# Products of w_out with two mixers' features beside the delta rule's norm and gate, and the modulation's columns spread anew

## The chip, the cores and the metric

The kernel runs on one core of a Trainium2 chip. The metric is the device time of one execution in microseconds (us). The time before is the median of 3 runs. Where the text speaks of levels of TensorE's clock, it means the granted clock that the profile shows: 1.00 is 2.4 GHz and 0.50 is 1.2 GHz.

## The reference, cut to what matters

The reference runs two blocks over 256 positions of width 1024, in float32. Only the seams that the change touches are shown.

```python
# first block, one layer
z = rms_norm(h, pre_mix_norm) @ w_in
o_rw  = rwkv7_mixer(...)      # delta rule: 384 features, group norm and gate at its end
o_nsa = nsa_mixer(...)        # sparse attention: 384 features
o_s5  = s5_mixer(...)         # state space: 256 features
mix = concatenate([o_rw, o_nsa, o_s5]) @ w_out          # 1024 x 1024
h = h + rms_norm(mix, post_mix_norm)
f = conv_ffn(rms_norm(h, pre_ffn_norm), w_up, conv_w, conv_b, w_down)
h = h + rms_norm(f, post_ffn_norm)
e = rms_norm(p @ w_ple, ple_norm); h = h + sigmoid(h @ w_ple_gate) * e
# second block: 112 columns of 128 modulation values, used as shifts, scales and gates
mod = silu(c) @ ada_w + ada_b       # 2 layers x 48 columns, and 16 for the keys and values
x = x + g1 * pool_mixer(...);  x = x + g2 * conv_ffn(...)      # layer 0
x = x + g1 * dilated_attention(...);  x = x + g2 * conv_ffn(...)  # layer 1
```

## The kernel before, in words

Activations lie transposed: 8 blocks of 128 features on the partitions, 256 positions along the free dimension. A linear layer is computed in three products of float32r halves. Each input is split into a rounded part `R` and a rest `L`, each weight tile `raw` into `wr` (a cast on ScalarE, L214) and `wl` (a difference on VectorE, L215), and `mm3` (L223 to L227) adds wr·R, wr·L and wl·R in one bank of PSUM. One output block of 128 features with 8 input blocks is 24 such instructions. Weights come over SP's queue in tiles of 512 KB, through 4 raw buffers and 2 buffers each of `wr` and `wl` in the mixers' stage.

The order on each engine is not written out by hand: a planner that simulates the engines orders the instructions by priority and readiness; `high_priority` lifts a block, `manual_schedule` keeps an engine's instructions of a block in their written order, and `issue_after(x)` keeps an instruction behind `x` on its engine. Once planned, each engine works strictly in that order.

**The mixers' stage** runs the delta rule (`rwkv`, lifted), the sparse attention (`nsa`) and the state space (`s5`, `s5_out`) beside each other. The delta rule ends in a chain of small products (`uprod`, L1017). Then come its group norm and gate (L689 to L698): `O` is centred by a product with `cen`, squared on ScalarE, summed per head by 12 small products, raised to the power -0.5 on POOL (L1040, 12 columns at once), spread by products (`head_bcast`), and VectorE multiplies by the spread factor (L695), adds `bon` (L696), multiplies by the gate `gv` (L697) and splits into `R[0..2]`, `L[0..2]`. `R[3..5]` are the sparse attention's features, `R[6..7]` the state space's.

**`post`** (L1156) follows with w_out: 8 output blocks, each with all 8 input blocks in turn, beginning with the delta rule's block 0. Of each block ScalarE writes a scaled copy `F` (L1164) and a square (L250); POOL adds the squares up (L254), and only the last two go through a product with ones. `rstd` turns the sums into the norm's factor (L270, POOL's power at L272, a spread by products). Then VectorE scales F and adds it to `xT` (L1175, L1177), each block's squares are summed by products with ones (32 instructions), a second `rstd` follows, and `norm_split` makes the next layer's inputs. The products of `w_ple` (`ple_vec`) and then `w_up` come next.

**The modulation** has 112 columns, which are made beside other work in two ways. `ada(n)` (L1127) loads 512 KB on SP's queue and makes one column by a VectorE instruction over 1024 elements (L1138); hooks call it after each output block at a rate from the tuple `ADA`. `ada_rows(n)` (L1083) makes four columns ("a row") by four loads of 512 KB through 3 buffers `adw` and 64 TensorE instructions, which are planned behind the last linear product; then ScalarE copies the row, two products turn it, and VectorE adds the bias (L1079). `ROWS` says how many rows stand at each place. The order of the columns is fixed: 0 to 63, then 96 to 111, then 64 to 95. `attention_layer` needs columns 104 to 111 for `gk` (L1376), the gain of the inputs `raw_x` of keys and values; `modv` makes at once whatever is missing.

Of the kernel before, what the change touches and what calls it, by code (L numbers as in the profile page):

```python
# [9 lines left out]
F32 = mybir.dt.float32  # L10
# [7 lines left out]
T = 256  # L18
# [10 lines left out]
ADA = (0,.5,2,.5,1.25,2,3.25,.75)  # L29
# [3 lines left out]
SKIP_W, SKIP_R, SKIP_A, SKIP_A2, SKIP_O = 480, 192, 0, 0, 0  # L33
# [7 lines left out]
ROWS = (1,2,0,0,1)  # L41
# [93 lines left out]
class Net:  # L135
# [46 lines left out]
    def setup(self):  # L182
# [10 lines left out]
        self.ones1 = self.const([128, 1], "ones1")  # L193
        nc.vector.memset(self.ones1, 1.0)
        self.mhalf = self.const([128, 12], "mhalf")
        nc.vector.memset(self.mhalf, -0.5)
        self.mod = self.const([128, 112], "mod")
# [3 lines left out]
        self.skip(self.cp, SKIP_W)  # L201
# [158 lines left out]
    def first(self):  # L360
# [11 lines left out]
        self.mixers(self.rstd(st, self.rcol))  # L372

    def mixers(self, rb):
        tc, a = self.tc, self.a
        with tc.tile_pool(name="mx", bufs=1) as mx, tc.tile_pool(name="mxp", bufs=2, space=PSUM) as self.px:
# [10 lines left out]
            if ORDER:  # L387
                self.fillq[0].clear(), self.fillq[1].clear()
                for c in ORDER:
                    if c == "u":  # L390
                        self.mix_u()
                    elif c == "r":
                        with tc.high_priority():
                            self.rwkv()
                    else:
                        for _ in dict(w=self.mix_nsa, s=self.s5, S=self.s5_out, c=self.nsa_cmp, n=self.nsa)[c]():
                            pass
                return
            self.mix_u()
            with tc.high_priority():  # L400
                self.rwkv()
# [89 lines left out]
    def rwkv(self):  # L491
# [45 lines left out]
        inv = self.head_stat(sq, 1.0, 1e-24, ALU.max)  # L537
# [99 lines left out]
        if not ORDER:  # L637
            self.fillq[0].append(self.nsa())
            self.fillq[1].append(self.s5_out())
# [43 lines left out]
        for q in self.fillq:  # L683
            self.drain(q)

        Oc, sq = t3("t4"), t3("sq3")
        for j in range(3):
            pc = rp()
            self.mm(pc[:, 0:T], self.cen, O[:, j])  # L689
            nc.scalar.activation(sq[:, j], pc[:, 0:T], AF.Square)  # L690
            nc.scalar.activation(Oc[:, j], pc[:, 0:T], AF.Identity, scale=self.vcol("rw_gn_w", j))
        inv = self.head_stat(sq, 1.0 / 64, GN_EPS, None)
        for j in range(3):
            ib = self.head_bcast(inv, j)
            nc.vector.tensor_tensor(Oc[:, j], Oc[:, j], ib, op=ALU.mult)  # L695
# [941 lines left out]
```

## Time and profile before

| | us |
|---|---|
| median of 3 runs | 1275.24 |
| lowest and highest | 1268.41, 1276.17 |
| profiled execution | 1271.01 |
| its span | 1269.1 |
| TensorE busy in the span | 1188.2 (94%) |
| VectorE, ScalarE, POOL busy | 940.1, 682.2, 99.8 |
| bytes moved | 247.19 MB |

The profile shows one execution. Its times count from the first instruction to the last; the remaining 1.9 us lie around the span. TensorE's busy time overstates its work where matmuls queue up or the clock is at its lower level, so a stretch is judged by three things together: what TensorE waited for, the granted clock, and the distance from one product to the next.

### The profile page before, as it was taken

The numbers are of one execution on the slowest core, as the hardware profiler recorded it, in microseconds if no ns is written. First come the engines' busy times: TensorE is split into PE (matmuls) and PEld (weight loads), VectorE is DVE, ScalarE is ACT, GpSimd is POOL, SyncE is SP. The second block draws the span as 40 slices with busy tenths as digits, with TensorE's granted clock in tenths as the row PEclk, the third lists the DMA queues.
The fourth block names the chain that finished last, engine by engine and source line by source line (L and its number), as shares of the span: only waits on it lengthen the run. The fifth ranks groups of instructions, "written<-read, shape, count | busy, mean of one in ns | idle before, by whom it ended". The sixth has DMA issues, their size and how long they took to land. (4 is left out here: it accounts for less than half of the span.)

```text
span 1269.1 us, 26242 instructions
## 1 busy us (share of the span) xinstructions
PE 1188.2 (94%) x10574; PEld 1119.6 (88%) x10574; DVE 940.1 (74%) x1847; ACT 682.2 (54%) x1194; POOL 99.8 (8%) x125
## 2 busy tenths in 40 slices
PE   5997899999999988888999998999999999999996
PEld 4985676899999988888999897999999998999996
DVE  7899646479999757788999866757574757877753
ACT  7633634556665535555665546455655466755541
POOL 0023200220000101220000010000000001000010
PEclk9998898889999988989999998999999999999998
DMA  8521300557668774367888783766464633666651
GB/s 282 159 86 51 119 34 4 189 203 256 219 235 299 258 265 160 124 238 260 313 309 283 284 312 116 286 219 218 165 218 151 229 116 106 204 192 203 211 184 34
DMA packets 71547, 247.19 MB, mean 195 GB/s; under 512 B 8192, under 2 KB 10496, under 8 KB 71424
## 3 DMA queue, kind: packets, MB, share of 16 engines
q1 hardware_dynamic: 71136, 244.72, 55.8%
q8 instruction: 83, 1.36, 0.4%
q10 hardware_dynamic: 288, 0.79, 0.2%
q14 instruction: 40, 0.33, 0.1%
HBM read 244.42 MB, written 1.05 MB: 193 GB/s over the span
## 5 line engine op out<-in xcount | busy, mean ns | idle before, releaser
L215 DVE TENSOR_TENSOR wl<-raw,wr 128x1024 fp32r<-128x1024 f32 (+3 forms) x348 | 412.0, 1190 | 145.4 <-ACT wr L214 143.5
L214 ACT CAST wr<-raw 128x1024 fp32r<-128x1024 f32 (+3 forms) x348 | 350.9, 1014 | 303.0 <-PE acc L226 242.9
L225 PE MATMUL acc<-R,wr 128*128 128x256 f32 x1472 | 413.5, 283 | 7.4 <-ACT wr L214 5.6
L227 PE MATMUL acc<-R,wl 128*128 128x256 f32 x1472 | 414.1, 282 | 2.7 <-DVE wl L215 2.6
L226 PE MATMUL acc<-L,wr 128*128 128x256 f32 x1472 | 414.4, 282 | 0.0
L225 PEld LDWEIGHTS acc<-R,wr 128*128 128x128 f32 x1472 | 280.0, 191 | 11.9 <-ACT wr L214 6.1
L227 PEld LDWEIGHTS acc<-R,wl 128*128 128x128 f32 x1472 | 280.0, 191 | 6.0 <-DVE wl L215 3.7
L226 PEld LDWEIGHTS acc<-L,wr 128*128 128x128 f32 x1472 | 282.1, 192 | 2.1 <-issue 1.4
L227 PE MATMUL acc<-aR,wl 128*128 128x256 f32 x608 | 168.6, 280 | 7.0 <-DVE wl L215 7.0
L225 PE MATMUL acc<-aR,wr 128*128 128x256 f32 x608 | 167.7, 281 | 6.0 <-ACT aR L282 5.3
L226 PE MATMUL acc<-aL,wr 128*128 128x256 f32 x608 | 168.6, 280 | 0.5 <-DVE aL L283 0.5
L1138 DVE SCALAR_TENSOR_TENSOR adw<-adw,cond 128x1024 f32<-128x1024 f32 x96 | 117.5, 1228 | 37.4 <-DMA adw<-in_ada_dram 36.0
L227 PEld LDWEIGHTS acc<-aR,wl 128*128 128x128 f32 x608 | 114.9, 190 | 8.0 <-DVE wl L215 8.0
L254 POOL TENSOR_TENSOR sq<-sq,sq 128x256 f32<-128x256 f32 x48 | 51.2, 1066 | 892.5 <-ACT sq L250 585.0
L225 PEld LDWEIGHTS acc<-aR,wr 128*128 128x128 f32 x608 | 114.4, 190 | 6.6 <-ACT aR L282 5.4
L226 PEld LDWEIGHTS acc<-aL,wr 128*128 128x128 f32 x608 | 115.7, 191 | 0.7 <-DVE aL L283 0.7
L225 PE MATMUL acc<-raw_x,wr 128*128 128x256 f32 (+1 forms) x320 | 92.5, 289 | 2.0 <-ACT wr L214 1.0
L226 PE MATMUL acc<-raw_x,wr 128*128 128x256 f32 (+1 forms) x320 | 92.6, 289 | 1.6 <-DVE raw_x L319 1.5
L227 PE MATMUL acc<-raw_x,wl 128*128 128x256 f32 (+1 forms) x320 | 92.6, 290 | 0.8 <-DVE wl L215 0.7
L242 PE MATMUL acc<-wr,raw_x 128*128 128x256 f32 x384 | 68.7, 281 | 0.4 <-DVE V L1439 0.4
L227 PEld LDWEIGHTS acc<-raw_x,wl 128*128 128x128 f32 x320 | 61.9, 194 | 2.7 <-issue 1.5
L225 PEld LDWEIGHTS acc<-raw_x,wr 128*128 128x128 f32 x320 | 61.5, 192 | 3.1 <-ACT raw_x L318 1.5
(416 smaller groups left out, 1711.8 us busy)
## 6 DMA issues: line engine op xcount, KB each, us to landing
adw<-in_ada_dram SPq DMA_DIRECT2D x96, 512.0 KB, 5.8
raw<-in_ffn_w_up_dram SPq DMA_DIRECT2D x88, 512.0 KB, 4.4
raw<-in_w_up_dram SPq DMA_DIRECT2D x44, 512.0 KB, 3.9
raw<-in_ffn_w_down_dram SPq DMA_DIRECT2D x32, 512.0 KB, 4.5
raw<-in_attn_w_q_dram SPq DMA_DIRECT2D x24, 512.0 KB, 6.7
raw<-in_w_k_dram SPq DMA_DIRECT2D x24, 512.0 KB, 3.6
raw<-in_w_v_dram SPq DMA_DIRECT2D x24, 512.0 KB, 3.9
raw<-in_w_in_dram SPq DMA_DIRECT2D x19, 512.0 KB, 3.6
```

The lines of the kernel that those rows point to most:

```text
L214: nc.scalar.copy(wr, raw)
L215: nc.vector.tensor_sub(wl, raw, wr[:].bitcast(F32))
L225: mm(out, wr, xr, start=start, stop=False)
L226: mm(out, wr, xl, start=False, stop=False)
L227: self.last_mm = mm(out, wl, xr, start=False, stop=stop).ins
L242: self.nc.tensor.matmul(out, lhsT, rhs, start=start, stop=stop)
L254: nc.gpsimd.tensor_tensor(sq, sq, self.sqsum, op=ALU.add)
L1138: nc.vector.scalar_tensor_tensor(w, w, 1.0, self.cond, op0=ALU.mult, op1=ALU.mult, accum_out=self.mod[:, i:i + 1])
```

## The change

The products with w_out leave `post` and move into a new function `mix_out` within the mixers' stage. Four banks of PSUM hold the eight output blocks, two to a bank. The products with input blocks 6, 7 and 3 of outputs 0 to 3 (`a67`, `a3`), then of outputs 4 to 7 (`b67`, `b3`), then those with blocks 4 and 5 (`k4`, `k5`) are placed between the steps of the delta rule's norm and gate; those with blocks 0 to 2 (`c`) come last, two outputs at a time. The weights are loaded in 12 pieces of other shapes, whose rows are 512 to 1536 bytes long; six are split into the two wr/wl buffers and six into tiles whose last use by the delta rule lies before. The gate's product is drawn ahead (bon·gv and Oc·gv before the factor is there), POOL's power is taken in three instructions of 4 columns, and the squares of all eight outputs are summed by products with ones (`pre=False`). Modulation: `ADA` is lower in the second block's first FFN and its w_down (1.25 to 1, 2 to 1.5 per output) and in the attention (3.25 to 3), there are two rows in place of one ahead of the attention, and the last FFN makes half a column per output. Pools `mx`, `mxp` and `wpm` get `reuse_waits="tile"`, a pad is gone, and `rawt` is 32 columns longer.

```diff
-ADA = (0,.5,2,.5,1.25,2,3.25,.75)
+ADA = (0,.5,2,.5,1,1.5,3,.75,.5)
-ROWS = (1,2,0,0,1)
+ROWS = (1,2,0,0,2)
...
-        with tc.tile_pool(name="mx", bufs=1) as mx, tc.tile_pool(name="mxp", bufs=2, space=PSUM) as self.px:
+        with tc.tile_pool(name="mx", bufs=1, reuse_waits="tile") as mx, tc.tile_pool(name="mxp", bufs=2, space=PSUM, reuse_waits="tile") as self.px:
...
+    def mix_out(self):
...
+        pz = [self.psum("acc", self.nacc) for _ in range(2)] + [self.psum("ms", MSB) for _ in range(2)]
+
+        def weights(m0, mn, k0, kn, tags=None):
+            n = mn * kn * 128
+            raw = self.rawload(self.a["w_out"][m0:m0 + mn, :, k0 * 128:(k0 + kn) * 128].rearrange(
+                "m p (k f) -> p m k f", k=kn), [128, mn, kn, 128])
+            if tags is None:
+                wr, wl = (self.wp.tile([128, mn, kn, 128], F32R, name=self.uid(t), tag=t, bufs=self.nw)[:] for t in ("wr", "wl"))
+            else:
+                w = [self.mxt([128, n * 2 // len(tags)], t, F32R) for t in tags]
+                wr, wl = (t.rearrange("p (m k f) -> p m k f", m=mn, k=kn) for t in (w[0][:, 0:n], w[-1][:, -n:]))
+            nc.scalar.copy(wr, raw)
+            nc.vector.tensor_sub(wl, raw, wr.bitcast(F32))
+            return wr, wl, m0, mn, k0, kn
+
+        out = lambda m: pz[m // 2][:, m % 2 * T:(m % 2 + 1) * T]
+
+        def products(w, m, ks=None):
+            wr, wl, m0, _, k0, kn = w
+            for k in range(kn):
+                self.mm3(out(m), wr[:, m - m0, k], wl[:, m - m0, k], self.R[:, k0 + k], self.L[:, k0 + k],
+                         k0 + k == 6 and m % 2 == 0, k0 + k == 2 and m % 2 == 1)
+
+        def early(w, anchor):
+            with tc.issue_after(anchor):
+                for m in range(w[2], w[2] + w[3]):
+                    products(w, m)
+
+        a67, a3 = weights(0, 4, 6, 2), weights(0, 4, 3, 1)
+        c = [weights(0, 2, 0, 3, ("e0", "e1")), weights(2, 2, 0, 3, ("t6", "Kt"))]
+        nc.vector.tensor_tensor(bon, bon, gv, op=ALU.mult)
+        early(a67, self.chain)
+        Oc, sq = t3("t4"), t3("sq3")
+        with tc.high_priority():
+            for j in range(3):
+                pc = self.psum("mx", 2)
+                last = nc.tensor.matmul(pc[:, 0:T], self.cen, O[:, j], start=True, stop=True).ins
+                nc.scalar.activation(sq[:, j], pc[:, 0:T], AF.Square)
+                nc.scalar.activation(Oc[:, j], pc[:, 0:T], AF.Identity, scale=self.vcol("rw_gn_w", j))
+        early(a3, last)
+        with tc.high_priority():
+            v, last = self.head_sums(sq, 1.0 / 64, GN_EPS)
+        nc.vector.tensor_tensor(Oc, Oc, gv, op=ALU.mult)
+        k4 = [weights(0, 4, 4, 1, ("t0", "t1")), weights(4, 4, 4, 1, ("t2", "t5"))]
+        c += [weights(4, 2, 0, 3, ("PB",)), weights(6, 2, 0, 3, ("PK",))]
+        b67, b3 = weights(4, 4, 6, 2), weights(4, 4, 3, 1)
+        early(b67, last)
+        early(b3, last)
+        with tc.manual_schedule(engines={mybir.EngineType.DVE}):
+            inv = self.tmp([128, 2, 6], "hr")
+            for j in range(3):
+                with tc.high_priority():
+                    h = slice(2 * j, 2 * j + 2)
+                    nc.gpsimd.tensor_tensor(inv[:, :, h], v[:].rearrange("p (a h) -> p a h", a=2)[:, :, h],
+                                            self.mhalf[:, 0:4].rearrange("p (a h) -> p a h", a=2), op=ALU.pow)
+            for j in range(3):
+                with tc.high_priority():
+                    ib = self.head_bcast(inv[:].rearrange("p a h -> p (a h)"), j)
+                    nc.vector.tensor_tensor(Oc[:, j], Oc[:, j], ib, op=ALU.mult)
+                    nc.vector.tensor_tensor(Oc[:, j], Oc[:, j], bon[:, j], op=ALU.add)
+                    self.split(Oc[:, j], self.R[:, j], self.L[:, j])
+            k5 = [weights(4 * i, 4, 5, 1) for i in range(2)]
+        for w in k4 + k5:
+            early(w, self.last_bc)
...
+        F = self.mxt([128, KB, T], "z9")
+        st = self.psum("st", 1)
+        for m in range(KB):
+            if m % 2 == 0:
+                products(c[m // 2], m)
+                products(c[m // 2], m + 1)
+            nc.scalar.activation(F[:, m], out(m), AF.Identity, scale=self.vcol("post_mix_norm", m))
+            self.sq_stat(st, out(m), m, pre=False)
+        return self.post_add(F, self.rstd(st[:, 0:2]), True)
...
-        self.ffn_up(a["ffn_w_up1"], None, False, "ffn_conv_w_2", "ffn_conv_b_2", 1, ps)
+        self.ffn_up(a["ffn_w_up1"], lambda m: self.ada(ADA[8]), False, "ffn_conv_w_2", "ffn_conv_b_2", 1, ps)
...
-        with tc.tile_pool(name="wo", bufs=1, reuse_waits="tile") as n.fp:
-            st = n.post(a["w_out"], n.R, n.L, n.vcol("post_mix_norm", 0, 8), KB, stat=True)
...
-    n.rawt = rt.tile([128, KB, 2, T + 32], F32R, name="raw_x")
+    n.rawt = rt.tile([128, KB, 2, T + 64], F32R, name="raw_x")
```

`post_add` is the second half of `post` before (L1171 to L1186), unchanged in what it does.

## Rows read from the trace of the kernel before

**Rows 1.** Page: busy time, share of the span, instructions of TensorE.
```profile
PE 1188.2 (94%) x10574; PEld 1119.6 (88%) x10574; DVE 940.1 (74%) x1847; ACT 682.2 (54%) x1194; POOL 99.8 (8%) x125
```

**Rows 2.** Stretches: length, busy time of each engine, granted clock, DMA share, GB/s.
```profile
206.50:213.00 6.50, 6.50 (x54) 4.95 (x50) 1.73 (x4) 3.72 (x10) 0.00 (x0) 1.00 0.01 3
213.00:215.60 2.60, 0.01 (x1) 0.00 (x0) 0.17 (x1) 0.00 (x0) 2.30 (x3) 0.67 0.01 3
215.60:224.10 8.50, 8.30 (x46) 7.28 (x47) 4.78 (x14) 3.56 (x5) 0.08 (x2) 0.50 0.10 31
224.10:243.90 19.80, 19.76 (x172) 19.55 (x172) 7.36 (x6) 10.93 (x20) 6.14 (x6) 1.00 0.46 161
243.90:248.80 4.90, 1.88 (x15) 1.52 (x14) 1.55 (x5) 1.17 (x3) 0.71 (x1) 0.92 0.70 245
248.80:256.00 7.20, 6.97 (x32) 6.88 (x32) 4.91 (x14) 3.85 (x8) 0.00 (x0) 0.50 0.51 199
```

**Rows 3.** Timeline of POOL: start, length, instruction, and the idle time before it.
```profile
213.30 2.28 POOL L1040 TENSOR_TENSOR hr<-hv,mhalf 128x12 f32<-128x12 f32 x1 [66.33 <-DVE hv L1036]
...
245.83 0.71 POOL L272 TENSOR_TENSOR rr<-rv,mhalf 128x2 f32<-128x2 f32 x1 [2.78 <-DVE rv L270]
```

**Rows 4.** Timeline of TensorE between the delta rule's end and w_up.
```profile
215.63 2.83 PE L242 MATMUL mx<-cst,hr 128*64 128x128 f32 x24 [2.62 <-POOL hr L1040]
...
243.94 0.50 PE L242 MATMUL st<-ones,sq 128*128 128x1 f32 x4
244.94 0.60 PE L242 MATMUL st<-ones,sq 128*128 128x1 f32 x4 [0.50 <-ACT sq L250]
...
248.78 6.99 PE L242 MATMUL acc<-ones,sq 128*128 128x1 f32 x32 [1.48 <-ACT sq L250]
...
260.45 6.89 PE L242 MATMUL acc<-pT,raw 128*128 128x256 f32 x28
```

**Rows 5.** Timeline of ScalarE: casts of two neighbouring output blocks of w_out.
```profile
233.15 1.05 ACT L214 CAST wr<-raw 128x1024 fp32r<-128x1024 f32 x1 [1.02 <-PE acc L226]
...
235.87 1.05 ACT L214 CAST wr<-raw 128x1024 fp32r<-128x1024 f32 x1 [1.02 <-PE acc L226]
```

**Rows 6.** Timeline of VectorE: the gate's first product and its last split.
```profile
216.80 0.42 DVE L695 TENSOR_TENSOR t<-t,mx 128x256 f32<-128x256 f32 x1 [3.58 <-PE mx L242]
...
220.64 0.98 DVE L283 TENSOR_TENSOR L<-t,R 128x256 fp32r<-128x256 f32 x2
```

**Rows 7.** Timeline of SP's queue: the loads of w_ple.
```profile
240.93 3.42 SPq L488 DMA_DIRECT2D raw<-in_w_ple_dram  x2
```

**Rows 8.** Page: one group of loads, count, KB each, median us to landing.
```profile
raw<-in_w_up_dram SPq DMA_DIRECT2D x44, 512.0 KB, 3.9
```

**Rows 9.** Timeline of TensorE in the second block's first FFN: waits for VectorE.
```profile
593.34 0.39 PE L227 MATMUL acc<-R,wl 128*128 128x256 f32 x1 [2.20 <-DVE wl L215]
...
720.32 0.39 PE L227 MATMUL acc<-aR,wl 128*128 128x256 f32 x1 [1.54 <-DVE wl L215]
```

**Rows 10.** VectorE's groups in 553 to 735: count, busy us, mean ns, idle before.
```profile
L1138 DVE SCALAR_TENSOR_TENSOR adw<-adw,cond 128x1024 f32<-128x1024 f32 x35 | 42.4, 1219 | 8.2 <-DMA adw<-in_ada_dram 8.1
```

**Rows 11.** Timeline of TensorE at the attention's start.
```profile
764.43 1.52 PE L242 MATMUL acc<-adw,ccol 128*32 128x128 f32 x48
...
772.93 1.08 PE L242 MATMUL acc<-adw,ccol 128*32 128x128 f32 x16 [4.53 <-DMA adw<-in_ada_r_dram]
...
785.75 0.28 PE L225 MATMUL acc<-raw_x,wr 128*128 128x256 f32 x1
```

**Rows 12.** Timeline of VectorE at the attention's start: first use of gk.
```profile
778.25 0.47 DVE L297 SCALAR_TENSOR_TENSOR ny<-xT,gk,st 128x256 f32<-128x256 f32 x1
```

**Rows 13.** Timeline of TensorE where two rows stand before: first and last instruction.
```profile
459.17 1.52 PE L242 MATMUL acc<-adw,ccol 128*32 128x128 f32 x48
...
481.24 0.28 PE L242 MATMUL acc<-cst,row 128*128 128x4 f32 x2
```

**Rows 14.** A stretch of the last FFN, columns as in rows 2.
```profile
1100.00:1200.00 100.00, 100.00 (x884) 100.00 (x884) 76.56 (x125) 60.45 (x97) 0.00 (x0) 1.00 0.63 202
```

More of the change, by code (lines that the diff above doesn't have):

```diff
@@ L386, in mixers @@
             self.mix_rw()
[L387 to L401, printed above, removed]
+            self.fillq[0].clear(), self.fillq[1].clear()
+            for c in ORDER:
+                if c == "u":
+                    self.mix_u()
+                elif c == "r":
+                    with tc.high_priority():
+                        self.rwkv()
+                else:
+                    for _ in dict(w=self.mix_nsa, s=self.s5, S=self.s5_out, c=self.nsa_cmp, n=self.nsa)[c]():
+                        pass
+            return self.mix_out()
     def mix_rw(self):
@@ L1025, in uprod, with head_sums, head_stat @@
             self.fill(self.phase)
-    def head_stat(self, sq, scale, eps, op):
+    def head_sums(self, sq, scale, eps):
+        nc = self.nc
+        st = self.psum()
+        for j in range(3):
+            for h in range(2):
+                last = nc.tensor.matmul(st[:, h * 6 + 2 * j:h * 6 + 2 * j + 2], sq[:, j, h * 128:(h + 1) * 128], self.hsel,
+                                        start=True, stop=True).ins
+        v = self.tmp([128, 12], "hv")
+        nc.vector.tensor_scalar(v, st[:, 0:12], scale, eps, op0=ALU.mult, op1=ALU.add)
+        return v, last
+    def head_stat(self, sq):
         nc = self.nc
@@ L1047, in head_bcast @@
                 c = h * 6 + 2 * j + i
-                self.mm(pb[i * 64:(i + 1) * 64, h * 128:(h + 1) * 128], r[:, c:c + 1].to_broadcast([128, 64]), self.ident)
+                self.last_bc = self.nc.tensor.matmul(pb[i * 64:(i + 1) * 64, h * 128:(h + 1) * 128],
+                                                     r[:, c:c + 1].to_broadcast([128, 64]), self.ident, start=True, stop=True).ins
         return pb[:, 0:T]
@@ L1167, in post, with post_add @@
                 hook(m)
-        if not stat:
-            self.ada_rows(ROWS[1])
-        rb = self.rstd(st[:, 0:2])
+        self.ada_rows(ROWS[1])
+        self.post_add(F, self.rstd(st[:, 0:2]), False)
+    def post_add(self, F, rb, stat):
+        nc = self.nc
         st = self.psum("acc", self.nacc) if stat else None
@@ L1500, in build @@
     psum = lambda name: tc.tile_pool(name=name, bufs=1, space=PSUM, reuse_waits="tile")
-    with tc.tile_pool(name="wpm", bufs=1) as n.wp, psum("psm") as n.ps:
+    with tc.tile_pool(name="wpm", bufs=1, reuse_waits="tile") as n.wp, psum("psm") as n.ps:
         n.nraw, n.nw, n.nacc = RAWM, WM, 2
         n.setup()
-        n.first()
-        if upto < 4:
-            return n
-        with tc.tile_pool(name="wo", bufs=1, reuse_waits="tile") as n.fp:
-            st = n.post(a["w_out"], n.R, n.L, n.vcol("post_mix_norm", 0, 8), KB, stat=True)
+        st = n.first()
         n.dump("x1", n.xT)
```

43 lines of the change are left out of this document (14 added, 29 removed).

## The prediction

> **What bounds the kernel now.** The page comes first: TensorE is busy 94% of the span [rows 1], so only a stretch in which it waits or runs at its lower clock can give time back. The table of stretches shows one such place where the change is made. From 206.5 to 213.0 us TensorE is busy at 1.00; then it stands still for 2.60 us; the next 8.50 us are busy but at 0.50, and from 224.1 on it is at 1.00 again [rows 2]. The timeline names the cause: the products that spread the norm's factor wait 2.62 us for POOL's power of 12 columns, which takes 2.28 us [rows 3, 4]. The w_out products begin only behind that, with the delta rule's block 0, so the gate and the lower clock both lie on the path. The last sum of squares ends at 245.54 (0.60 us from 244.94, where TensorE had waited 0.50 for ScalarE's square [rows 4]). The stretch to judge is thus 206.50 to 245.54, 39.04 us. Afterwards comes a chain of two norms, with TensorE busy 1.88 of 4.90 us and then at 0.50 on small sums [rows 2], which the change keeps as it is.
>
> **Products of w_out.** Their number stays 192. Two neighbouring casts stand 2.72 us apart [rows 5], one output block of 24, so 0.1133 us each at the full clock and 21.8 us in all. What changes is when they may start: 120 of them (blocks 3 to 7, 13.6 us) need nothing of the norm and gate. They cover the 2.60 us, and while TensorE is fed the clock has no idle stretch before it to fall after, so I count the 8.30 busy us at 0.50 as 4.15. Removed: 2.60 + 4.15 = 6.75 us. The norm and gate themselves take from 213 to 221.6 (the last split, 0.98 us from 220.64 [rows 6]); the products to hide them amount to 13.6 us, so this chain is no longer the bound.
>
> **Sums of squares.** Before, POOL adds the squares and 8 small instructions remain; now there are 32. Four took 0.50 us at the full clock [rows 4], so 32 take 4.0 and 24 more cost 3.0 us. Those of the last pair fall in a wait: as two outputs share a bank, ScalarE can only read output 6 when output 7 is done, two copies and squares after the last product instead of one, about 0.85 us more.
>
> The sum from below: 6.5 us to 213 [rows 2]; 24 spreading products at half of 2.83 [rows 4], 1.4; 21.8 of products; sums of outputs 0 to 3, 2.0; tail of 0.2 + 1.7 + 0.5. That is 34.1 us against 39.04, a gain of 4.9. From above: 39.04 - 6.75 + 3.0 - 0.5 (sums now inside the tail) + 0.85 = 35.6, less some of the 0.8 us by which the first blocks waited for their R: a gain of 3.4 to 4.2. I take **4.4**, near the middle.
>
> **Casts, loads and the gate.** The casts have the same number of elements. ScalarE spent 8 x 1.05 us [rows 5]; as 12 pieces it pays a few starts more. That is under 1.5 us, with ScalarE busy 3.72 of 6.50 us and VectorE 1.73 of 6.50 ahead of 213 [rows 2], so it is hidden; if the cover fails, a cast in front of a step of the norm delays it by at most one cast, 1.05. Three gate products of 0.42 us [rows 6] leave the chain and two longer ones go into idle VectorE time. The power: three of 4 columns lie between 0.71 each (2 columns) and 2.28 (12 columns) [rows 3]; linear between these, about 1.0, so the first factor is there some 1.2 us sooner and the last 0.8 later. Both are covered by the early products. SP's queue gets 12 loads in place of 8 for the same 4 MB. The DMA engines are 0.01 to 0.10 busy between 206 and 224 [rows 2], so I cost them at nothing, but the second wave of weights needs raw buffers that casts must free first (rival 2). The trace has no load with rows this short; the nearest lands in a median of 3.9 us [rows 8].
>
> By the Trainium skill (DMA: Bandwidth & Descriptors, "Why small descriptors are slow (HBM only)") each packet pays some three fixed cycles; as an estimate from that page a 512-byte row loses 3 of 19 cycles, about 0.6 us on such a load. That sentence would add nothing to the sum and leans a little towards rival 2; no run shows it yet.
>
> **Modulation.** In the second block's first FFN and its w_down there are 8 columns fewer (20 in place of 25, 9 in place of 12). VectorE made 35 there at 1.22 us [rows 10], and four TensorE waits for VectorE stand there, from 2.20 to 1.54 us, 5.7 together [rows 9]. Bounds: 0 and 5.7. I take the share of the columns, 8 of 37, **1.2 us gained**. The ten columns of the last FFN add 12 us to VectorE, busy 76.6 of 100 there with TensorE at 100 [rows 14]: hidden, with 0.5 as the other bound. Two columns fewer in the attention: nothing, TensorE is full there.
>
> The attention's start is the price. Counting the columns by the rates, 80 are ready ahead of it before (104 to 111 among them, so gk waits for no row); now 72, and the two rows make exactly the missing 104 to 111. So gk, at the front of VectorE's second normalization, waits for both rows, and behind it on VectorE stand eight inputs raw_x. Three loads are there at once, the fourth landed so that its products came at 772.93, 8.5 us after the first [rows 11], and a second round of three buffers puts the last loads near 782, gk near 784 instead of 778.25 [rows 12]. raw_x is first used at 785.75 [rows 11]; VectorE has two instructions of some 0.47 [rows 12] per block, about 0.8 us as they overlap a little, and TensorE three products, 0.34, so the last block would make TensorE wait about 3 us. Bounds: 0 (48 products with R of the next pair, 5.4 us, can be put in) and 8.2 (the other place with two rows took 22.07 us from first to last [rows 13], which would be 786.5 here). I take **1.0 us lost**, since the planner sees the loads.
>
> Sum: 4.4 + 1.2 - 1.0 = 4.6 us less. The profiled execution took 1271.01, so 1266.4. That execution lies 4.2 below the median of 1275.24 and 2.6 above the lowest run; the mean of all four is 1272.7, from which 4.6 less is 1268.1. Between the two I predict **1267**.
>
> **Rivals.**
> 1. *The next layer's start moves into the hole.* The casts of w_out would end with the gate, near 221, so the loads of w_ple, issued at 240.93 when the last cast was over [rows 7], can come then, and their products (6.89 us for 28 of 32 [rows 4]) could run beside the two norms, where TensorE is idle 3.0 us of 4.9 and half speed thereafter [rows 2]. For: weights and banks come free earlier. Against: the rows' products planned ahead of them came only when the norm's bank was free, and the order is the planner's. Worth 6 us more: 1261. Chance 0.19.
> 2. *The early products wait for their weights.* b67 and b3 need raw buffers freed by casts into tiles that the delta rule holds to its end, and wr/wl buffers freed by a67 and a3; being in order on TensorE, a late load holds the norm's spreading products too. One landing (3.9 us [rows 8]) eats the 4.4 and leaves the sums' 3.0 partly unpaid: 1267 + 4 to 6, about 1272. Chance 0.18.
> 3. *The second row holds the attention.* If the planner puts nothing in and the row is as late as in rows 13, TensorE stands 8.2 us at the first raw_x, and such a wait has a lower-clock stretch behind it, worth 4.15 at the delta rule [rows 2]. 12.4 in place of 1.0: 1278, slower than before. It decides when gk comes later than about 781, from which on VectorE's pace no longer keeps ahead. Chance 0.11.
> 4. *The clock stays at 0.50 through the last products,* since they now alternate with one-column sums. The sums after the norm ran at 0.50 (6.99 us for 32) [rows 4]; 72 products and 32 sums at half speed would cost 8.2 + 3.0 more: 1278. Against: those sums stood between waits, these between products. Chance 0.06. The Trainium skill (TensorE: Matmul & The Clock Gate, "A second HAM failure mode: psum-queue depth-cycling") says that small idles between groups that cycle through banks can make the clock swing; by that rule this rival's time would hold, and the trace's 1.00 from 224.1 on, with one output per bank, does not show it.
>
> **How the numbers follow.** The forecast (1267, its own range 1262 to 1272) has 0.46. The range that leaves out 2 in 10 runs from 1256 (the better half of rival 1, and FFN waits gone wholly) to 1278 (rivals 3 and 4 at their middle). One per cent of 1275.24 is 12.8 us, about what a measurement can tell from no change: faster means under 1262.5, slower over 1288. Faster gets most of rival 1 and the low end of the forecast, 0.21; slower the tails of rivals 3 and 4, 0.04; the rest, 0.75, is within.
>
> **What would show it.** Right: no TensorE wait for POOL's power between 206 and 222, the granted clock at 1.00 from the delta rule's end to the last product, the last sum of squares near 241, and fewer waits for VectorE in the FFN. Wrong: a wait for wl or a load before b67 or c (rival 2), w_ple's products ahead of the second norm (rival 1), a wait at the first raw_x (rival 3), 0.50 in the last 72 products (rival 4). Since all of this moves well under 1%, a planner's order that differs far from the change, ahead of 206 or in the attention, could outweigh it either way.

## The result, and the profile after

Against the kernel before on the same chip the change measured 1255.12 us to 1271.83, a ratio of 0.9888 (95% interval 0.984 to 0.9935, four runs each). Measured again with five rounds it was 1261.59 to 1266.82, 0.9958 (0.993 to 0.9986). The forecast, 4.6 us less, is a ratio of 0.9964: inside the second interval, outside the first. The first median, 1255.12, stands 0.9 us below the predicted range of 1256 to 1278, and its gain of 1.1% is what the prediction called faster, with a chance of 0.21. The second, 1261.59, stands inside the range; the kernel before was faster too in that session, and a gain of 0.4% is below the one per cent that the prediction took for about what a measurement can tell. The profiled executions took 1257.43 (span 1255.6) and 1266.19 (span 1264.4).

The page of the changed kernel, busy time of TensorE and the others, as in [rows 1]:

```profile
PE 1184.4 (94%) x10664; PEld 1116.8 (89%) x10664; DVE 934.8 (74%) x1839; ACT 680.5 (54%) x1197; POOL 95.8 (8%) x121
```

The stretches of the changed kernel from the end of the delta rule's chain (200.4) to the second norm, columns as in [rows 2]:

```profile
200.40:212.40 12.00, 12.00 (x100) 10.03 (x96) 6.60 (x11) 6.53 (x14) 0.00 (x0) 1.00 0.46 154
212.40:216.00 3.60, 3.60 (x33) 3.31 (x31) 0.93 (x3) 0.95 (x2) 2.98 (x3) 1.00 0.03 5
216.00:223.60 7.60, 7.46 (x69) 6.50 (x69) 4.84 (x11) 1.74 (x4) 0.00 (x0) 1.00 0.13 36
223.60:234.80 11.20, 11.20 (x98) 11.20 (x98) 0.00 (x0) 4.26 (x12) 0.00 (x0) 1.00 0.69 258
234.80:238.20 3.40, 2.29 (x20) 2.04 (x18) 0.16 (x1) 1.39 (x4) 0.80 (x3) 0.87 0.00 0
238.20:248.00 9.80, 8.16 (x36) 7.78 (x36) 6.42 (x19) 4.87 (x10) 0.00 (x1) 0.50 0.08 23
```

From 200.4 to 234.8 TensorE is never at 0.50 and stands still for 0.14 us. While POOL takes its power (second row, 2.98 busy), TensorE is full; the 2.60 us of standstill and the half clock of [rows 2] are gone. POOL's timeline, to be held against [rows 3]:

```profile
212.71 2.98 POOL L737 TENSOR_TENSOR hr<-hv,mhalf 128x4 f32<-128x4 f32 x3 [68.86 <-DVE hv L1096]
...
237.40 0.69 POOL L271 TENSOR_TENSOR rr<-rv,mhalf 128x2 f32<-128x2 f32 x1 [21.71 <-DVE rv L269]
```

Three powers of 4 columns take 2.98 us, 1.0 each, as interpolated.

**Where the time went.** The instructions on VectorE that begin each norm's factor (`rv`) cut the program into stages which both kernels have. The table gives each stage's mean and its lowest and highest over profiles of kernels that share the code and order in question (the experiments below included): for the first five lines three kernels with the old order there and five profiles with the new one, for the rest six with the old modulation and six with the new. In the last line each time is a level that one to four profiles show, and the difference is that of the lowest two; between the means it would be +3.8.

| stage | old, us | new, us | new - old | forecast |
|---|---|---|---|---|
| start to the chain's last product | 205.1 (204.0 to 206.3) | 198.9 (197.8 to 200.4) | -6.2 | 0 |
| on to the last sum of squares of w_out | 39.7 (39.3 to 40.1) | 36.8 (36.8 to 36.9) | -2.9 | -4.4 |
| two norms and w_ple, to its norm | 28.9 (28.8 to 29.0) | 31.0 (30.8 to 31.3) | +2.1 | 0 |
| first FFN and the gate behind it | 232.5 (227.3 to 236.6) | 226.4 (226.1 to 227.3) | -6.1 | 0 |
| pool mixer | 68.2 (67.9 to 68.3) | 68.9 (67.9 to 70.4) | +0.7 | 0 |
| second block's first FFN | 190.0 (185.8 to 197.1) | 188.1 (185.2 to 191.1) | -1.9 | -1.2 |
| attention | 310.7 (309.0 to 313.9) | 314.7 (313.8 to 315.7) | +4.0 | +1.0 |
| last FFN | 179.9 or 183.7 or 186.3 | 181.2 or 187.5 | +1.3 | 0 |

The largest line is one that the forecast had at nothing: the delta rule's chain, whose products the change leaves as they are, ends 6.2 us sooner.

**The chain.** ScalarE's timeline of the kernel before, the loads of a function table (1.28 us each) and the chain's copy behind them:

```profile
136.84 1.28 ACT L479 ACT_TABLE_LOAD   x1
...
138.43 1.28 ACT L822 ACT_TABLE_LOAD   x1
...
140.58 1.28 ACT L479 ACT_TABLE_LOAD   x1
...
142.16 1.28 ACT L822 ACT_TABLE_LOAD   x1
...
143.85 0.46 ACT L1022 COPY t<-mx 128x384 f32<-128x384 f32 x1
```

TensorE's timeline of the same kernel, the product that needs this copy:

```profile
144.36 0.91 PE L1017 MATMUL mx<-t,t 64*64 64x64 f32 x24 [3.72 <-ACT t L1022]
```

The sparse attention's sigmoids (L479, 18 gates for each half of the positions) and exponentials (L822) take turns, so the function changes four times in 7 us and the copy stands behind all of it. ScalarE's timeline of the changed kernel:

```profile
134.43 1.28 ACT L882 ACT_TABLE_LOAD   x1
...
139.16 1.28 ACT L474 ACT_TABLE_LOAD   x1
...
141.65 0.48 ACT L1082 COPY t<-mx 128x384 f32<-128x384 f32 x1
...
142.67 1.28 ACT L882 ACT_TABLE_LOAD   x1 [0.53 <-DVE z L886]
```

Here the planner has put the two sigmoids side by side, and the copy comes ahead of the next load. TensorE's wait of 3.72 us is gone, and with it the stretch at the lower clock from 145.6 to 152.4. The chain has 960 such products in both kernels, so they can be matched one to one. The changed kernel is 0.3 us ahead at the 179th (134.0 against 134.3), 3.7 at the 251st (141.0 against 144.7), 6.2 at the 323rd (147.6 against 153.8) and 5.9 at the last: all of the lead arises here. The Trainium skill (ScalarE: Activation LUTs, "What ACT_TABLE_LOAD costs") gives 1283 ns for the load and 2.66 us for a switch with its drain; the trace agrees with the load, but the exponential at 139.72 follows the load at 138.43 by 1.29 us, so the switch costs 1.3 here, and the measurement decides. The rule of the Trainium skill (ScalarE: Activation LUTs, "Table sets: the hidden batching unit") to batch activations by set is what the new order happens to follow: three loads stand between 130 and 143 us rather than five.

### The profile page after: what moved, and what is told of

The parts are those of the page before. It is cut to its first block, busy times and chain, and to the rows that moved or that the text cites. A ratio compares the mean times of both kernels' runs of the same rounds, so it can differ in the third digit from the quotient of the medians.

```text
span 1255.6 us, 26442 instructions
## 1 busy us (share of the span) xinstructions
PE 1184.4 (94%) x10664; PEld 1116.8 (89%) x10664; DVE 934.8 (74%) x1839; ACT 680.5 (54%) x1197; POOL 95.8 (8%) x121
## 5 line engine op out<-in xcount | busy, mean ns | idle before, releaser
L214 DVE TENSOR_TENSOR wl<-raw,wr 128x1024 fp32r<-128x1024 f32 (+3 forms) x340 | 400.8, 1182 | 128.8 <-ACT wr L213 128.0
L213 ACT CAST wr<-raw 128x1024 fp32r<-128x1024 f32 (+3 forms) x340 | 343.0, 1014 | 266.1 <-PE acc L225 210.8
L224 PE MATMUL acc<-R,wr 128*128 128x256 f32 x1424 | 400.2, 282 | 5.5 <-ACT wr L213 5.2
L226 PE MATMUL acc<-R,wl 128*128 128x256 f32 x1424 | 399.9, 281 | 3.9 <-DVE wl L214 3.7
L225 PE MATMUL acc<-L,wr 128*128 128x256 f32 x1424 | 399.5, 281 | 0.0
L224 PEld LDWEIGHTS acc<-R,wr 128*128 128x128 f32 x1424 | 270.3, 190 | 9.8 <-ACT wr L213 5.5
L226 PEld LDWEIGHTS acc<-R,wl 128*128 128x128 f32 x1424 | 271.2, 191 | 7.6 <-DVE wl L214 5.0
L225 PEld LDWEIGHTS acc<-L,wr 128*128 128x128 f32 x1424 | 270.3, 190 | 1.8 <-issue 1.5
L1208 DVE SCALAR_TENSOR_TENSOR adw<-adw,cond 128x1024 f32<-128x1024 f32 x92 | 113.0, 1232 | 43.9 <-DMA adw<-in_ada_dram 43.5
L253 POOL TENSOR_TENSOR sq<-sq,sq 128x256 f32<-128x256 f32 x42 | 46.4, 1104 | 867.3 <-ACT sq L249 702.2
```

The lines of the kernel that those rows point to most:

```text
L213: nc.scalar.copy(wr, raw)
L214: nc.vector.tensor_sub(wl, raw, wr[:].bitcast(F32))
L224: mm(out, wr, xr, start=start, stop=False)
L225: mm(out, wr, xl, start=False, stop=False)
L226: self.last_mm = mm(out, wl, xr, start=False, stop=stop).ins
L253: nc.gpsimd.tensor_tensor(sq, sq, self.sqsum, op=ALU.add)
```

## The experiments

All ratios are to the kernel before, in the same session, with 95% intervals; the medians of before were 1266.82, 1267.47 and 1268.94 in the three sessions.

**The changed kernel again.**

> The changed kernel once more, with five rounds. Theory: it stands at 0.985 to 0.992 of the kernel before (1253 to 1262 us), and in a second profile the delta rule again ends 5 to 6 us earlier and the w_out stretch is again 2 to 3 us shorter, since both follow from the instructions' order. Rival: the first four runs were lucky by several us: 0.993 to 0.997, and parts of the 14 us between the two profiles (the 4 us in the gate stage above all) are not there in a second profile.

Measured 1261.59, 0.9958 (0.993 to 0.9986). In time the rival holds. The chain's end (199.4) and the w_out stretch (36.9) came back as in the first profile, as the theory had it, and so did the gate (42.4 us, 41.5 in the first); the last FFN did not, 187.5 rather than 181.2, although TensorE waits there 2.0 us in both and the granted clock is 1.00 in both. The stretches of 20 us, changed kernel first and then its second profile, and the products in them (count, shortest, median and longest duration in ns):

```profile
1103.00:1123.00 20.00, 20.00 (x179) 20.00 (x178) 17.06 (x31) 12.43 (x21) 0.00 (x0) 1.00 0.66 234
...
L224 PE MATMUL acc<-R,wr x60: 276/276/276, 1102.8 to 1122.8; 128*128 128x256 f32 x60
```

```profile
1106.00:1126.00 20.00, 20.00 (x172) 20.00 (x171) 16.84 (x30) 11.56 (x19) 0.00 (x0) 1.00 0.62 223
...
L224 PE MATMUL acc<-R,wr x57: 281/281/281, 1105.9 to 1125.7; 128*128 128x256 f32 x57
```

The same instructions come 111.7 ns apart in one execution and 116.3 in the other. Each execution switches between the two paces several times. A stage of 180 us at the slower pace is 6 to 7 us longer, and no wait shows it. So a difference of a few us in a dense stage (the FFN lines of the table) means little, and lines with much waiting, whose ranges lie apart, mean more.

**The modulation alone**, in the kernel before:

```diff
-ADA = (0,.5,2,.5,1.25,2,3.25,.75)
+ADA = (0,.5,2,.5,1,1.5,3,.75,.5)
...
-ROWS = (1,2,0,0,1)
+ROWS = (1,2,0,0,2)
...
-        self.ffn_up(a["ffn_w_up1"], None, ...
+        self.ffn_up(a["ffn_w_up1"], lambda m: self.ada(ADA[8]), ...
```

> The kernel before with the change's modulation alone: ADA and ROWS as in the changed kernel, and the half column per output in the last FFN. Theory: the gain of the change does not come from here. In the profiles of before and after the second block's FFN gains 3.5 us, the start of the attention loses 3.4 and the last FFN loses 1.4, together +1 or so; this kernel stands within 3 us of the kernel before (1269 to 1275 us against 1272). Rival: the modulation brings a good part of the gain, because fewer VectorE instructions of 1024 elements stand ahead of the weights' splits: 1264 to 1268 us.

Measured 1272.93, 1.0043 (1.0012 to 1.0074): slower by 5.4 us, more than the theory's 3, which the interval still holds, and the rival falls. The attention took 315.7 us, and a wait of 1.08 us for VectorE's `wl` appeared early in the last FFN.

**All but the modulation**, the reverse edit in the changed kernel:

> The changed kernel with the old modulation (ADA, ROWS, no hook in the last FFN). Theory: nearly the whole gain lies ahead of 500 us (the delta rule 5.7 us, the w_out stretch 2.4, the second norm 0.9, the gate of the per-layer embedding 4.1): 1256 to 1261 us against 1272 of the kernel before, the start of the attention waiting 4.5 us as it did before and not 6.9. Rival: half of the gain needs the modulation's columns: 1263 to 1267 us.

Measured 1258.01, 0.9939 (0.9916 to 0.9963), the best ratio of these twelve runs. The gain, 7.7 us by the ratio, is smaller than the theory's 11 to 16 and of the rival's size, but not for the rival's reason: without the new columns the time is lower, not higher. In its profile the attention takes 309.0 us, the chain ends at 197.8. The two halves, +0.43% and -0.61%, add up to -0.18%; the whole gave -0.42%, and the intervals cover this gap.

**The table loads alone**, in the kernel before; the gates are made with the exponential:

```diff
...
-            nc.scalar.activation(sg[:, th], ..., AF.Sigmoid, scale=self.rcol[:, th:th + 1])
+            nc.scalar.activation(sg[:, th], ..., AF.Exp, scale=nrc[:, th:th + 1])   # nrc = -rcol
+        nc.vector.tensor_scalar(sg, sg, 1.0, None, op0=ALU.add)
+        nc.vector.reciprocal(sg, sg)
```

> The kernel before with one edit: the sparse attention's 18 gates (L479) are made as 1/(1+exp(-x)) with ScalarE's exp and two small VectorE instructions, so that four of the five loads of a function table between 134 and 143 us go, and nothing of the change is in it. Theory: the delta rule's copy at 143.85 us no longer stands behind four loads of 1.28 us, TensorE's wait of 3.72 us at 144.4 shrinks below 1 us and the half clock after it goes: the chain ends 4 to 6 us earlier, 1266 to 1268 us against 1272. Rival: the copy then waits for the sparse attention's exponentials or VectorE instead, and the chain's end moves by less than 1.5 us: 1270.5 to 1272 us.

Measured 1263.98, 0.997 (0.9944 to 0.9995), below 1 as the theory wants: 3.8 us by the ratio, against 4 to 6. The profile is plainer. Stretches of the kernel before, and of this one:

```profile
140.00:147.00 7.00, 3.28 (x54) 2.06 (x49) 4.01 (x15) 6.89 (x16) 1.42 (x2) 0.90 0.32 116
147.00:154.00 7.00, 7.00 (x91) 4.44 (x90) 5.42 (x16) 4.21 (x9) 0.00 (x0) 0.61 0.45 150
```

```profile
140.00:147.00 7.00, 7.00 (x130) 4.76 (x122) 6.32 (x21) 4.41 (x12) 1.41 (x2) 1.00 0.64 228
147.00:154.00 7.00, 5.88 (x140) 5.15 (x141) 4.91 (x14) 3.17 (x7) 0.00 (x0) 1.00 0.91 330
```

TensorE does 270 instructions in these 14 us rather than 145, at 1.00 throughout, and the chain ends at 198.7, 7.6 us sooner and where the changed kernel has it, with not a line of the change in it. TensorE's order is the same in both kernels up to 144.8 us of this profile and 153.5 of the kernel before, beyond the product that waited for the copy, while ScalarE's differs from its first dropped load on (136.84). So it is shown, in the kernel before, that ScalarE's order ends the chain sooner. That it is the cause in the changed kernel too rests on the timelines above and on the lead that arises at the same products.

**The gates through the exponential in the changed kernel:** the same three lines.

> The changed kernel with the sparse attention's gates made through the exponential, as was done to the kernel before: two more table loads go. Theory: the changed kernel's order had already taken the loads off the delta rule's copies, so that little is left: the chain ends 0 to 1.5 us earlier than the 198 to 200 us of the changed kernel, no change in the time (0.990 to 0.996 of the kernel before). Rival: the loads cost their 2.6 us in full in the changed kernel, and the chain ends near 196.

Both were wrong. The chain ended at 211.8, 12.9 us later than the changed kernel's mean, and the ratio was 0.997 (0.9939 to 1.0001). TensorE's timeline of the changed kernel, and of this one:

```profile
150.54 1.61 PE L1077 MATMUL mx<-t,t 64*64 64x64 f32 x48 [1.08 <-DVE t L1082]
```

```profile
150.55 2.72 PE L1081 MATMUL mx<-t,t 64*64 64x64 f32 x46 [2.86 <-ACT t L1086]
```

ScalarE's timeline of this kernel ahead of that product, and the stretches that follow:

```profile
146.75 1.57 ACT L698 CAST wr<-raw 128x1024 fp32r<-128x1024 f32 x2 [1.77 <-DMA raw<-in_w_out_dram]
148.34 1.28 ACT L797 ACT_TABLE_LOAD   x1
...
150.03 0.47 ACT L1086 COPY t<-mx 128x384 f32<-128x384 f32 x1
```

```profile
150.00:160.00 10.00, 9.45 (x142) 8.56 (x144) 3.58 (x10) 2.01 (x5) 0.00 (x0) 0.50 0.34 93
160.00:170.00 10.00, 10.00 (x133) 9.15 (x133) 3.06 (x6) 1.22 (x3) 0.00 (x0) 0.50 0.15 41
170.00:187.00 17.00, 16.29 (x185) 14.40 (x185) 5.12 (x16) 3.88 (x8) 0.00 (x0) 0.50 0.08 25
```

The chain's product starts at 150.5 in both, behind two casts of w_out, which wait for their load, a table load (the gelu's) and the copy. What differs is that TensorE, whose order is the same up to there, had run out of other work 1.8 us sooner, and so stood still 2.86 us rather than 1.08. After that the chain runs at 0.50 until 187. The wait itself delayed nothing: the 371st product of the chain starts at 151.1, against 150.9 in the changed kernel. Behind it, at half the clock, the chain falls back: at the 635th product, up to which the changed kernel stayed at 1.00, it is 8.8 us late (173.3 against 164.5), and at the last 11.4 (12.9 against the mean). Taking table loads away is thus no gain in itself: it helped in the kernel before, where it closed TensorE's wait, and hurt here, where it opened one.

**No overlap:** the 72 products with blocks 6, 7 and 3 of the changed kernel pass behind the last spread product.

```diff
-        early(a67, self.chain)
...
-        early(a3, last)
...
-        early(b67, last)
-        early(b3, last)
...
-        for w in k4 + k5:
+        for w in [a67, a3, b67, b3] + k4 + k5:
```

> The changed kernel with the products of w_out's input blocks 6, 7 and 3 (72 of them) behind the delta rule's last spread product, like those of blocks 4 and 5, so that nothing of w_out runs beside the norm. All else stays, ScalarE's order in the delta rule too. Theory: the overlap is what shortens the stretch; without it the power's wait and the half clock come back: from the chain's last product to the last sum 39 to 42 us rather than 36.9 (39.3 in the kernel before), the chain's end as in the changed kernel (198 to 201 us). Rival: the overlap brings nothing, since the products in between delay the norm by as much as they fill: 36.5 to 37.5 us.

Measured 0.9969 (0.9936 to 1.0002). The chain ended at 198.6 and the last sum came 39.35 us behind it: the theory. TensorE's timeline and the stretch from the wait on:

```profile
207.99 1.47 PE L1113 MATMUL mx<-cst,hr 128*64 128x128 f32 x10 [1.85 <-POOL hr L733]
```

```profile
207.50:211.20 3.70, 3.21 (x25) 2.36 (x26) 1.53 (x4) 0.40 (x1) 2.40 (x3) 0.55 0.06 24
```

The wait for POOL is back, and half clock behind it, though for less time (3.4 us, from 207.9 to 211.3) than the 8.5 us of [rows 2]. So the overlap alone is worth 2.5 us.

**POOL's sums** in the changed kernel (`pre=False` left out):

> The changed kernel with the squares of w_out's outputs added up by POOL again, as in the kernel before, and only the last two summed by products. Theory (the forecast's price): the twelve more sums cost TensorE 3.0 us, so that the stretch from the chain's end to the last sum falls from 36.9 to 34 us. Rival: the sums lie beside ScalarE's copies and squares, which set the pace at the end; POOL's chain of adds takes their place, and the stretch stays at 36.5 to 38 us.

Measured 0.9971 (0.9942 to 1.0). The stretch fell to 35.7, by 1.1 us, between the two. TensorE's timeline shows why the 3.0 us did not come back whole:

```profile
232.96 1.05 PE L241 MATMUL st<-ones,sq 128*128 128x1 f32 x8 [1.70 <-POOL sq L253]
```

The last sums wait 1.70 us for POOL. The time of the whole did not get better.

**The queries first.** Of the eight loads' products of the two modulation rows, the last five stand behind the first two blocks of query products; the keys' gain and norm follow the rows.

```diff
-        self.ada_rows(ROWS[4])                     # end of second()
+        rows = self.row_steps(ROWS[4])             # attention_layer, three steps
...
+            self.qk0 = self.att_qk(0, (0,))
+            for _ in rows:
+                pass
             gk = self.scaled_gain("gk", ...
```

> The changed kernel with one edit at the attention's start: the first three of the eight loads' products of the modulation rows stay where they are, the other five pass behind the first two blocks of query products, which need no row. Theory: the loss there is TensorE's order, not the late gain of the keys: in the changed kernel TensorE waits 4 to 5 us and more for loads adw at half clock while the queries' inputs are ready. Then the queries begin about 5 us after the last sum rather than 15, the first values are copied 31 to 34 us after that sum rather than 39, and the kernel gains 4 to 8 us on the changed kernel. Rival: the keys' gain gk comes later by as much, the wait goes to the first key product, and the values stand 37 to 40 us after the sum: no change.

Measured 0.9951 (0.9915 to 0.9986), no change; the attention took 317.4 us rather than 314.7, the first values stood 42.8 us after the last sum rather than 39.2. TensorE's timeline of the changed kernel, which was taken as the reason:

```profile
746.96 1.52 PE L241 MATMUL acc<-adw,ccol 128*32 128x128 f32 x48
...
755.60 2.21 PE L241 MATMUL acc<-adw,ccol 128*32 128x128 f32 x32 [4.67 <-DMA adw<-in_ada_r_dram]
...
763.55 0.59 PE L241 MATMUL acc<-cst,row 128*128 128x4 f32 x2 [0.44 <-ACT row L1145]
764.40 0.58 PE L224 MATMUL acc<-R,wr 128*128 128x256 f32 x1 [0.26 <-DVE mod L1149]
...
775.20 0.28 PE L224 MATMUL acc<-raw_x,wr 128*128 128x256 f32 x1
```

and of the reordered one, with ScalarE's row behind it:

```profile
754.49 0.58 PE L224 MATMUL acc<-R,wr 128*128 128x256 f32 x1 [4.75 <-ACT R L284]
...
773.91 0.50 PE L224 MATMUL acc<-raw_x,wr 128*128 128x256 f32 x2 [1.51 <-ACT raw_x L284]
```

```profile
750.54 3.50 ACT L1532 ACTIVATE bt<-dt 128x512 f32<-128x512 f32 x9 [3.36 <-DMA dt<-in_dist_dram]
```

The queries begin 9 us sooner after the last sum, and would begin sooner still if ScalarE did not make nine tiles `bt` first. But the keys' gain comes 24.6 us after that sum rather than 15.2, and the first key product 25.9 rather than 26.0. The rival holds, except that the values came later still than its 37 to 40: moving the queries only moved the wait. The same reordering with the old modulation:

> The changed kernel with the old modulation (one row, the old rates) and the reordered attention start of the run above. Theory: both edits add up: the first values 28 to 31 us after the last sum against 34.4 with the old modulation alone, and a time 12 to 15 us below the kernel before. Rival: with one row the queries waited little (8.9 us from the last sum), so the order brings less than 2 us: 8 to 9 us below the kernel before.

Measured 0.9961 (0.9934 to 0.9988), 4.9 us below the kernel before: neither. The values came 33.0 us after the sum rather than 34.4, the small gain of the rival, but the attention took 311.0 us rather than 309.0, and the time is no better than with the old modulation alone (0.9939).

**A better version.** The old modulation and the exponential in the changed kernel, and the same with POOL's sums:

> The changed kernel with the old modulation and the gates through the exponential, as a candidate for a better version. Theory: the old modulation gives back the 4.6 us of the attention's start, the exponential next to nothing: 0.991 to 0.995 of the kernel before, 1256 to 1261 us, below both kernels. Rival: what the old modulation gave alone (0.994) was partly the spread of the runs, and this stands with the changed kernel at 0.995 to 0.997.

> As the run above, and the squares of w_out's outputs added by POOL again. Theory: 1.1 us less in the w_out stretch, as in the run with POOL's sums alone, so 0.990 to 0.994 of the kernel before. Rival: no difference that can be seen.

Measured 0.9973 (0.9947 to 0.9999) and 0.9999 (0.9972 to 1.0026): neither theory holds. Both chains ended near 209.9, with 34 us at 0.50 behind a wait (2.40 and 2.20 us) up to 149.8, as in the run with the exponential alone. So no combination beats the changed kernel with the old modulation, 0.9939, and even that interval touches the changed kernel's own.

**The layout alone**, in the kernel before, every engine's order unchanged:

```diff
-SKIP_W, SKIP_R, ... = 480, 192, ...
+SKIP_W, SKIP_R, ... = 0, 192, ...
...
-        with tc.tile_pool(name="mx", bufs=1) as mx, ...            # likewise mxp, wpm
+        with tc.tile_pool(name="mx", bufs=1, reuse_waits="tile") as mx, ...
...
-    n.rawt = rt.tile([128, KB, 2, T + 32], F32R, name="raw_x")
+    n.rawt = rt.tile([128, KB, 2, T + 64], F32R, name="raw_x")
```

> The kernel before with only the change's layout: the pools' reuse_waits, no pad, the longer rawt. Every engine's instructions stand in the same order as in the kernel before. Theory: no part of the gain comes from here, and this run shows how far two kernels with one and the same order differ by the spread of executions: within 0.3% of the kernel before, the chain's end at 205 to 206.5 us and the last sum 39.3 us behind it. Rival: waits on released memory were part of the gain, and the delta rule ends 3 us or more earlier.

Neither: 1276.93, 1.0071 (1.0043 to 1.0099). The chain ended at 204.0 and the stretch was 40.1, so this part of the layout is not where the gain is. (The change also swaps the places of a few small constants, `ones1` and `mod` among them; no run tries that alone.) But two kernels with one order differ by 0.7%. A dense stretch of its first FFN:

```profile
300.00:320.00 20.00, 20.00 (x171) 20.00 (x170) 19.35 (x36) 13.60 (x23) 0.00 (x0) 1.00 0.72 260
```

171 instructions in 20 us, and so it goes in most of this execution. Whether placement in memory makes the slower pace likelier was not settled; one kernel and one profile do not tell it. The intervals of the rounds do not contain this difference. It is larger than the 0.4% of the changed kernel and than most differences between the runs here, so whole times this near to each other decide little, and the argument rests on the stages. What the layout does to the time of the changed kernel itself, which has it too, no run shows.

## Why the prediction was right, and where not

**The sum was right by cancelling, which is luck.** It had -4.4, -1.2 and +1.0. The runs show -2.9, about 0 and +4.0 for these, and outside of them -6.2, +2.1, about -6 and +1.3. The last sentence of the prediction, that a planner's order ahead of 206 could outweigh the change, is what happened: the chain ended 6.2 us sooner.

**The w_out stretch: mechanism right, size not.** No wait for POOL, 1.00 from the chain's end to the last product, the early products no later than needed: all as forecast; the last sum came at 237 rather than near 241 because the chain ended sooner. Rivals 2 and 4 are out: TensorE's one gap in the stretch, at 222.2, is 0.14 us long, and no half clock stands among the 72 last products. The prediction held that the trace before has no load with rows as short as those of the new pieces. It has: eight of 128 KB for the pool mixer with rows of 1024 bytes, which landed in a median of 2.1 us, and two of 64 KB with rows of 512 (4.1 and 3.3). The new pieces with rows of 512 bytes landed in 2.8 to 4.7 us. What short rows cost by themselves these loads do not separate, since they differ in bytes as well.

What was mis-sized is the product term, 21.8 us. The sum from below gave 34.1, the profiles 36.8. From one start to the next the 192 products of the changed kernel take 24.5 us, which is the whole difference of 2.7; the other terms of the sum are off by 0.3 to 0.7 each and cancel. Of the distances 19 are 0.20 to 0.41 instead of 0.115; together these are 2.2 us over. Fifteen of them, 1.5 us, stand where TensorE changes between the products and small float32 work; the other four stand between products, at 212.4 and around the gap at 222.2. The rest, 0.5, is the pace of the products: 0.116 in place of 0.1133. TensorE's timeline of the changed kernel around one group of sums:

```profile
233.03 0.50 PE L241 MATMUL st<-ones,sq 128*128 128x1 f32 x4
233.39 0.36 PE L224 MATMUL ms<-R,PK 128*128 128x256 f32 x1
233.59 0.28 PE L225 MATMUL ms<-L,PK 128*128 128x256 f32 x1
...
234.88 2.24 PE L241 MATMUL st<-ones,sq 128*128 128x1 f32 x16
```

The first product after the sums takes 0.20 to the next start, the others 0.11 to 0.12. In this stretch the kernel before changes between the two kinds of work 2 times, the changed kernel 24 times; work that fills holes pays at their edges. The last row is the tail as forecast: 16 sums after the last product. The 3.0 us for the sums are about right as work (a group of four takes 0.36 and 0.08 more at the product behind it, and there are six groups more: 2.6), but POOL's way costs 1.70 of waiting, so that they lose only 1.1.

**Rival 1 did not come, and a little was lost instead.** The loads of w_ple do start early, at 223.3, but the products come after the second norm, at 252.8. In the kernel before, 38 products of a modulation row stood at 256.02, ahead of the second norm's spread, and covered POOL's power; now the row stands behind the spread, and TensorE waits 1.03 us at 248.96. TensorE's timeline of the kernel before, and of the changed kernel:

```profile
256.02 2.36 PE L242 MATMUL acc<-adw,ccol 128*32 128x128 f32 x38 [0.25 <-DVE rv L270]
```

```profile
248.96 1.22 PE L241 MATMUL st<-cst,rr 128*128 128x128 f32 x4 [1.03 <-POOL rr L271]
```

That is half of the +2.1; the other half was not traced.

**The FFN: nothing that can be told.** Four waits, those at 593 and 720 [rows 9] among them, were taken as 5.7 us, of which a share would go. In the changed kernel the first is still there, in full; of waits for VectorE as long as the other three (0.94 to 1.54 us) none is left, the longest being 0.25, which is the sign that the forecast named; and one for ScalarE has come:

```profile
579.48 0.38 PE L226 MATMUL acc<-R,wl 128*128 128x256 f32 x1 [2.10 <-DVE wl L214]
...
693.97 0.39 PE L224 MATMUL acc<-aR,wr 128*128 128x256 f32 x1 [1.18 <-ACT aR L281]
```

But in the changed kernel with the old modulation they are gone as well (0.64 us at most), so the new columns are not needed for that. With the old modulation the profiles run from 185.8 to 197.1, with the new from 185.2 to 191.1. The two paces of TensorE are larger than any effect of the columns.

**The attention: four times the price, at another place.** The forecast had the second row hold the first key product, with TensorE filled by queries until then. The planner put the queries themselves behind both rows: the first one comes 15.2 us after the last sum rather than 8.2, and the clock there is at 0.50 for 17.1 us in five of the six profiles with two rows (13.7 in the sixth), rather than 6.8 to 10.2 in the six with one. `gk` came 15.2 us after that sum, 2 sooner than forecast, and TensorE did not wait at `raw_x` at all. So rival 3 was right that the second row holds the attention and wrong on where; its 12.4 us shrank to 4.0.

**The last FFN: +1.3 rather than 0**, between profiles at the faster pace. The bound of 0.5 was too tight; a wait of 0.96 for `wl` at 1079 and what follows it stands in every profile with columns there.

**Open.** The first FFN and the gate, -6.1 between means. Over all profiles the ranges overlap: 227.3 to 236.6 in the four with the old w_out code, 219.2 to 234.0 in the ten with the new. The kernel before and the changed kernel ran the FFN at like paces (281 ns from about 275 to 410 us in both), and their difference there, 2.4, stands beside a wait of 2.59 us for `wl` at 424 that the changed kernel has not. The gate took 44 to 46 us in the four profiles with the old w_out code, and 39 to 43 in nine of the ten with the new (45.4 in the other); in the changed kernel the second row's products end 15 us after the first sum there rather than 18 to 20. So the shorter gate seems to come with that code; which instruction of it moved the planner was not tried alone.

## What to carry to other kernels

When a planner orders the engines, a change in one stage reorders the stages ahead of it. Read the neighbours of a long serial chain on every engine it uses: here what stood ahead of one copy on ScalarE, and how much work TensorE had left meanwhile, was worth 6 us in one direction and 13 in the other, more than the 2.9 of the stretch that the change was made for. Judge a change of under 1% by the distance between the same two instructions over several profiles, not by one pair of executions, and hold work that is to fill a hole against the cost of changing over at its edges.

## What the runs showed of the hardware

- At a granted clock of 1.00 TensorE has two paces, 111.7 and 116.3 ns between products of 128x256 (276 and 281 ns each), and switches during an execution; the layout run was near the slower one, 117, for most of its time. The Trainium skill (TensorE: Matmul & The Clock Gate, "Wait — 56ns, not 53.3ns?") puts the distance of matmuls at N / 2.4 GHz and about 2.5 ns more, which gives an estimate of 109.2 ns for 256 columns. Both paces are above it, and the measurement decides.
- With the exponential in the changed kernel, the granted clock fell to 0.50 in one wait of 2.86 us, 0.7 us before its end, and stayed there until 187, for 37 us, although TensorE was busy 36 of them, mostly with the chain's products of 64x64. After a wait of 1.12 us, in the kernel before with the exponential, it stayed at 1.00:

```profile
149.18 0.92 PE L1021 MATMUL mx<-t,t 64*64 64x64 f32 x24 [1.12 <-DVE t L1026]
```

- In the w_out stretch of the changed kernel the first float32r product after a group of small float32 instructions takes 0.20 to 0.23 us to the next start in eleven of twelve cases, against 0.115 between products (in the twelfth, a product alone between two groups, 0.31).
